# Where the splits of newly loaded weights stand in ScalarE's queue, and the order of the seven products of a hidden block, in a four-layer trunk

## The chip, the cores and the metric

The kernel runs on 1 core of one Trainium2 chip. The metric is the device time of one execution in microseconds (us), the median of the runs; lower is better. TensorE (PE) does the matmuls, VectorE (DVE), ScalarE (ACT) and GpSimd (POOL) the elementwise work, and SyncE (SP) issues most of the loads.

## The reference

The reference is a trunk of two layers, each a half-step SwiGLU feed-forward network (FFN), a mixer (a gated short convolution in the first layer, sparse attention in the second) and another half-step FFN. That makes six stages, numbered s = 0 to 5; stages 0, 2, 3 and 5 are the FFNs. Only they matter here:

```python
def swiglu(h, w_in, w_out):
    g, u = jnp.split(h @ w_in, 2, axis=-1)
    return (jax.nn.silu(g) * u) @ w_out

x = x + HALF * gate[:, 0, None, :] * swiglu(h, ffn_w_in[i, 0], ffn_w_out[i, 0])
```

Here x is 512 positions by 1024, w_in is 1024 by 5632 (2816 for g and 2816 for u) and w_out is 2816 by 1024, all in fp32.

## The kernel before, in words

**Splitting.** An fp32 operand goes through the matmul as two numbers, a high part and a low part. `split` (L163 and L164) makes them: ACT copies the value into the high part, and DVE subtracts that from the value for the low part. A product of two split operands takes three matmuls: high by high (L167), high by low (L168) and low by high (L169); in the rows of the profile the weight is the second name, so that `gu<-hhi,whi` has the weights' high part and `gu<-hhi,wlo` their low part.

**The hidden blocks.** An FFN has 22 hidden blocks of 128, in four groups (0 to 5, 6 to 11, 12 to 17, 18 to 21), called p = 0 to 3 below. Most blocks are done by `seven_products`: a block's two 1024 by 128 weight matrices (g and u) and the 512 positions are cut in halves, so that eight products of blocks become seven of sums of blocks. It is called 73 times: 16 times in the first FFN and 19 times in each of the other three. One call is a *pair* here. A product is 12 matmuls of 128x256 (4 blocks of the inner dimension by 3). Their names, by the stationary operand in the profile's rows:

- `a11` and `a12` take the newly loaded weights, split into `whi` and `wlo`;
- `b2·t2` takes `qbh`/`qbl`, `s1·t1` and `s3·t3` take `qah`/`qal`, the fourth-sum product takes `qdh`/`qdl`, and the last product takes `qch`/`qcl`. The tiles qa, qb and a are sums and quarters of the same weights, split in the same way. Of qb there are two sums, made by DVE at L661 and L662 from the raw weights.

Three PSUM banks of a pair are called gu. Each of them is read once by a copy on ACT in `copied` (L697): `e0` after a11, `e1` after b2·t2, `e3` after s1·t1. The product that next adds to the same bank has to wait for that copy: b2·t2 for e0, s3·t3 for e1, the fourth-sum product for e3. After that DVE adds (L708, L721, L725), ACT applies Silu (L726), and two DVE operations (L731, L732) make the hidden block af, which is split into ahi and alo.

The pairs overlap. A call returns two functions, `fourth` (the fourth-sum product with its add and Silu) and `last` (the last product, L731, L732 and the split of af), which the next call runs among its own products. The steady order on PE, with X for a pair and Y for the next, is: a11 of Y, fourth of X, a12 of Y, b2·t2 of Y, last of X, s1·t1 of Y, s3·t3 of Y. Only the second pair of a group runs fourth ahead of a11.

**Loads and buffers.** The raw weights (`wraw`, 512 KB), their high and low parts have three buffers each, shared with the weights of the output projection and of the next stage. SP issues the loads of raw weights (L656 in a pair, L186 elsewhere).

**After a group.** The group's blocks go through w_out into eight outputs y of 128x512, with weights by `ffn_out` (768 columns, L186), and L813 adds each to x. The first two outputs are begun ahead of the group's last block. The fourth group has no y phase: four weight pairs `ws` (two through the shared buffers, two through other tiles as th and tl) feed the products ty, and the first weights of the next stage are loaded there too (called nx0, of `in_cwi`, `in_ffi` or `in_nwi`).

**What sets the order.** The program is written for a scheduler that puts each engine's instructions in a fixed queue; `tc.high_priority()`, `tc.issue_after(...)` and `behind(...)` steer it. `tc.issue_after(ins)` puts what follows behind ins in a queue; it works on the instructions that ins's own engine gets. So behind a copy on ACT it places the high part and leaves the low part on DVE free. In before, the split of a pair's weights is placed in this way for a group's second pair only, behind the e1 copy of the first. `each` (called in `row` and after L813) gives DVE row sums of another stage's modulation weights (L147) to do beside.

Of the kernel before, what the change touches and what calls it, by code (L numbers as in the profile page):

```python
# [22 lines left out]
P = 128  # L23
# [3 lines left out]
KD = D // P  # L27
# [26 lines left out]
def decoder_kernel(ctx, tc, xT, cT, ng, adaw, adab, ffi, ffo, cwi, cw, cwo,  # L54
                   nwi, nwv, pos, w1, w2, qg, kg, nwo, rb, onehot, rowok, out):
    nc = tc.nc
# [394 lines left out]
        return weights(ffi[f, j, c], KD, P, own, held, to=to)  # L451


    def ffn_out(f, d, m, j0, j1, own=None):
        src = ffo[f, d:d + m, :, j0 * P:j1 * P].rearrange("d p c -> p d c")
        return weights(src, m * (j1 - j0), P, own)

    class Hidden:
        def __init__(self, es, bufs):
# [160 lines left out]
    def ffn(s, f, nrm, nxt, w0, ahead, extra=(), soon=()):  # L620
        with ExitStack() as es:
# [12 lines left out]
            def seven_products(j, later, before, copied_before, second):  # L634
                QT = KD * P // 2
                quart = lambda c, k: ffi[f, j, c].rearrange("p k n -> p (k n)")[:, k * QT:(k + 1) * QT]
                raw = wp.tile([P, 2, QT], F32, name="wraw", tag="wraw", bufs=3)
                whi = wp.tile([P, 2, QT], F32R, name="whi", tag="whi", bufs=3)
                wlo = wp.tile([P, 2, QT], F32R, name="wlo", tag="wlo", bufs=3)
                qa = next(sums)()  # L640
                a22 = tp.tile([P, T], F32, name="a22", tag="nacc", bufs=1) if j == nj and not first else tmp("a22")
                qb = [tmp("qb", tag="sq") for _ in range(2)] if first else swa.tile([P, 2, QT], F32, name="qb")
                qbs = qb if first else [qb[:, 0], qb[:, 1]]
                ah_, al_ = (sw.tile([P, 2, QT], F32R, name=f"qa{e}") for e in "hl")
                b2 = [sw.tile([P, QT], F32R, name=f"qb{e}") for e in "hl"]
                halves = qa if isinstance(qa, list) else [qa[:, 0], qa[:, 1]]
                nc.sync.dma_start(halves[0], quart(0, 0))
                nc.sync.dma_start(halves[1], quart(1, 1))
                a21 = quart(1, 0)
                if qa is halves:  # L650
                    for q in qa:
                        nc.gpsimd.dma_start(q, a21, accum_op=ALU.add)
                else:
                    nc.gpsimd.dma_start(qa, bass.AP(tensor=a21.tensor, offset=a21.offset, ap=[a21.ap[0], [0, 2], a21.ap[1]]),  # L654
                                        accum_op=ALU.add)
                nc.sync.dma_start(raw.rearrange("p a b -> p (a b)"), ffi[f, j, 0].rearrange("p k n -> p (k n)"))  # L656
                nc.sync.dma_start(a22, quart(1, 1))

                def operands(after=nullcontext):
                    with after(), behind(*hid.done) if first and copied_before else nullcontext():  # L660
                        nc.vector.tensor_tensor(qbs[0], halves[1], raw[:, 0], ALU.add)  # L661
                        nc.vector.tensor_tensor(qbs[1], qbs[0], raw[:, 1], ALU.add)  # L662
                    with tc.issue_after(copied_before.ins) if second else nullcontext():
                        split(raw, whi, wlo)
                    if qa is halves:
                        for n, q in enumerate(qa):
                            split(q, ah_[:, n], al_[:, n])
                    else:
                        split(qa, ah_, al_)
                    split(qbs[0], *b2)  # L670

                if j == nj and first:
                    with behind(*held_back):
                        operands()
                elif later:
                    with behind(*hid.done):
                        operands()
                else:
                    operands((lambda: behind(*nrm.done[1])) if j == nj else nullcontext)

                def product(o, w, b, begin=True):
                    for i in range(KD // 2):
                        c = slice(i * P, (i + 1) * P)
                        mh, ml = b(i)
                        mm3(o, w[0][:, c], w[1][:, c], mh, ml, begin and i == 0, i == KD // 2 - 1, skip_group_check=True)

                a11, a12 = [(whi[:, i], wlo[:, i]) for i in range(2)]
                s3, s1 = [(ah_[:, i], al_[:, i]) for i in range(2)]
                t1, t2, t3, t4 = nrm.blocks
                lo, hi = slice(0, HT), slice(HT, T)  # L690
                ox, oy, oz = psum("gu"), psum("gu"), psum("gu")
                e = sw.tile([P, 2, HT], F32, name="e", bufs=2)
                e3 = tmp("e3", HT, "xr")

                def copied(to, o):
                    with tc.high_priority():
                        return nc.scalar.activation(to, o[:, lo], AF.Copy)  # L697

                if second:
                    before[0]()  # L700
                product(ox[:, lo], a11, nrm.quarter(0, 0))
                copied(e[:, 0], ox)
                if not second:
                    before[0]()
                b4 = [sw.tile([P, QT], F32R, name=f"qd{e}") for e in "hl"]
                split(qbs[1], *b4)
                product(oz[:, lo], a12, nrm.quarter(1, 0))
                nc.vector.tensor_tensor(e[:, 0], oz[:, lo], e[:, 0], ALU.add)  # L708
                product(ox[:, lo], b2, t2, begin=False)
                copy = copied(e[:, 1], ox)  # L710
                before[1]()
                if second and late:
                    late.pop()
                    with tc.issue_after(hid.done[1].ins):
                        each()
                c22 = [sw.tile([P, QT], F32R, name=f"qc{e}") for e in "hl"]
                split(a22, *c22)
                product(oy[:, lo], s1, t1)
                copied(e3, oy)
                product(ox[:, lo], s3, t3, begin=False)  # L720
                nc.vector.tensor_tensor(e3, ox[:, lo], e3, ALU.add)  # L721

                def fourth():
                    product(oy[:, lo], b4, nrm.quarter(1, 1), begin=False)
                    nc.vector.tensor_tensor(e[:, 1], oy[:, lo], e[:, 1], ALU.add)  # L725
                    nc.scalar.activation(e, e, AF.Silu)  # L726

                def last():
                    product(ox[:, lo], c22, t4, begin=False)
                    af = tmp("af")  # L730
                    nc.vector.scalar_tensor_tensor(af[:, hi], e[:, 1], -1.0, e3, op0=ALU.mult, op1=ALU.mult)  # L731
                    nc.vector.scalar_tensor_tensor(af[:, lo], e[:, 0], -1.0, ox[:, lo], op0=ALU.mult, op1=ALU.mult)  # L732
                    keep(af)

                return (fourth, last), copy
# [33 lines left out]
                    hid.activate(os[2 * j], os[2 * j + 1])  # L769
            held_back = []  # L770
            copy, late = None, []
            for p, (j0, j1) in enumerate(FOUR):
                rest = none = (lambda: None,) * 2
                for j in range(max(j0, nj), j1):
                    rest, copy = seven_products(j, p and j == j0, rest, copy, copy and j == max(j0, nj) + 1)
                n = j1 - j0
# [13 lines left out]
                if not final:  # L790
                    begun = []
                    for d in range(KD):
                        if d < 2 and both:
                            if not d:
                                a = (hid.hi[j0:j1 - 1], hid.lo[j0:j1 - 1])
                                for dd in range(2):
                                    begun.append((ffn_out(f, dd, 1, j0, j1), psum("y")))
                                    project(begun[dd][1], begun[dd][0], 0, a, [(k, k) for k in range(n - 2)], True, False)
                                    if not dd:
                                        rest[1]()  # L800
                                for w, o in begun:
                                    project(o, w, 0, a, [(n - 2, n - 2)], False, False)
                                a = (hid.hi[j0:j1], hid.lo[j0:j1])
                                row()
                            w, o = begun[d]
                            project(o, w, 0, a, [(n - 1, n - 1)], False, True)
                        else:
                            w = ffn_out(f, d, 1, j0, j1)
                            if first and not p and d == 6:
                                held_back[:] = last_split  # L810
                            o = psum("y")
                            project(o, w, 0, a, [(k, k) for k in range(n)], True, True)
# [802 lines left out]
```

## Time and profile before

| | us |
|---|---|
| runs | 1907.12, 1908.41, 1909.41 (median 1908.41) |
| profiled execution | 1905.69 |
| its span | 1903.9 |
| PE busy | 1871.5 (98%) |
| DVE busy | 1516.9 (80%) |
| ACT busy | 951.1 (50%) |
| mean granted clock | 1.0 |

The span runs from the first to the last instruction on the core; what the execution took beyond it is 1.8 us. A timeline row has the start, the duration, the engine, the line, the operation with its output and inputs, and in square brackets the idle time of the engine ahead of it with what ended it. The matmuls overlap one another, so a row's 0.28 is not what a matmul costs; the distance between two starts is.

### The profile page before, as it was taken

Reading aid. Unit: us, or ns where it says so; the run is one execution under the profiler, and the core shown is the slowest. Engines: PE = TensorE matmul, PEld = TensorE weight load, DVE = VectorE, ACT = ScalarE, POOL = GpSimd, SP = SyncE. Lnnn points to the kernel's source line nnn. Section 1 sums busy time; section 2 is a strip of 40 time slices with the busy share of each in tenths; the row PEclk is TensorE's granted clock in tenths of the full one; section 3 lists DMA queues with packets and bytes.
Section 4 is the critical chain, followed back from the end, with each engine's and each line's share of the span. In section 5 each row is a group of like instructions: output and inputs, shape, how many; then the busy total and the mean of one; then the engine's idle time right before and its main releaser. Section 6 shows DMA issues by size and latency. Waiting matters only on the chain.

```text
span 1903.9 us, 34466 instructions
## 1 busy us (share of the span) xinstructions
PE 1871.5 (98%) x13293; PEld 1736.6 (91%) x13293; DVE 1516.9 (80%) x2792; ACT 951.1 (50%) x1679; POOL 250.5 (13%) x346
## 2 busy tenths in 40 slices
PE   7999999999999999999999999999999999999999
PEld 5989999988899899999989899999888789898989
DVE  8977878887797878788878878887898988585765
ACT  3445344532245454545635353554788856363542
POOL 0011111000011111100011111000454620010100
PEclk9999999999999999999999999999999999999999
DMA  8587767366656677774568676234332325474741
GB/s 326 179 241 188 227 175 252 122 222 243 243 161 172 202 197 230 191 248 107 145 210 216 200 200 211 85 110 130 82 99 80 90 72 143 125 201 115 200 121 63
DMA packets 126674, 324.77 MB, mean 171 GB/s; under 512 B 15515, under 2 KB 16651, under 8 KB 126508
## 3 DMA queue, kind: packets, MB, share of 16 engines
q1 hardware_dynamic: 95196, 242.85, 38.6%
q0 software_dynamic: 31312, 79.71, 18.2%
q8 instruction: 104, 1.70, 0.4%
q14 instruction: 62, 0.51, 0.1%
HBM read 313.85 MB, written 3.15 MB: 166 GB/s over the span
## 4 chain that ended last, share of the span: by engine, by line
PE 84%; DVE 8%; ACT 3%; DMA 2%; issue 2%; SPq 1%; DVEq 0%; ACTq 0%
PE gu L167 13%; PE gu L169 12%; PE gu L168 12%; PE y L167 7%; PE y L168 7%; PE y L169 7%; PE cv L167 2%; PE cv L169 2%; PE cv L168 2%; PE hs L168 2%; PE hs L169 2%; PE hs L167 2%; PE ty L168 2%; PE ty L169 2%; PE ty L167 2%
## 5 line engine op out<-in xcount | busy, mean ns | idle before, releaser
L163 ACT ACTIVATE whi<-wraw 128x1024 fp32r<-128x1024 f32 (+2 forms) x261 | 252.7, 976 | 266.7 <-PE y L168 88.5
L164 DVE TENSOR_TENSOR wlo<-wraw,whi 128x1024 fp32r<-128x1024 f32 (+2 forms) x261 | 294.8, 1134 | 44.8 <-ACT whi L163 44.0
L168 PE MATMUL y<-alo,whi 128*128 128x512 f32 x576 | 224.3, 389 | 0.0
L167 PE MATMUL y<-ahi,whi 128*128 128x512 f32 x576 | 224.3, 389 | 0.0
L169 PE MATMUL y<-ahi,wlo 128*128 128x512 f32 x576 | 224.2, 389 | 0.0
L147 DVE CUSTOM_DVE_ANT_0 adaraw<-adaraw,cond,adabs 128x1024 f32<-128x1024 f32 x144 | 185.6, 1305 | 12.9 <-DMA adaraw<-in_adaw 12.6
L167 PE MATMUL gu<-hhi,whi 128*128 128x256 f32 x696 | 192.9, 277 | 0.0
L169 PE MATMUL gu<-hhi,wlo 128*128 128x256 f32 x696 | 192.5, 277 | 0.0
L168 PE MATMUL gu<-hlo,whi 128*128 128x256 f32 x696 | 192.4, 277 | 0.0
L654 POOL DMA_DIRECT2D qa<-in_ffi x70 | 84.5, 1207 | 697.5 <-DMA qa<-in_ffi 259.4
L167 PE MATMUL gu<-th,qah 128*128 128x256 f32 x584 | 161.5, 276 | 1.4 <-ACT e L697 1.4
L169 PE MATMUL gu<-th,qal 128*128 128x256 f32 x584 | 161.2, 276 | 0.0
L168 PE MATMUL gu<-tl,qah 128*128 128x256 f32 x584 | 161.2, 276 | 0.0
L697 ACT ACTIVATE e<-gu 128x256 f32<-128x256 f32 x219 | 82.5, 377 | 127.5 <-PE gu L169 126.7
L167 PEld LDWEIGHTS gu<-hhi,whi 128*128 128x128 f32 x696 | 130.7, 188 | 1.0 <-DVE af L732 0.4
L168 PEld LDWEIGHTS gu<-hlo,whi 128*128 128x128 f32 x696 | 130.6, 188 | 0.5
L169 PEld LDWEIGHTS gu<-hhi,wlo 128*128 128x128 f32 x696 | 130.7, 188 | 0.0
L169 PEld LDWEIGHTS y<-ahi,wlo 128*128 128x128 f32 x576 | 108.1, 188 | 22.9
L167 PEld LDWEIGHTS y<-ahi,whi 128*128 128x128 f32 x576 | 108.2, 188 | 21.7
L168 PEld LDWEIGHTS y<-alo,whi 128*128 128x128 f32 x576 | 108.1, 188 | 21.5
L167 PEld LDWEIGHTS gu<-th,qah 128*128 128x128 f32 x584 | 109.6, 188 | 1.6 <-ACT e L697 1.6
L169 PEld LDWEIGHTS gu<-th,qal 128*128 128x128 f32 x584 | 109.7, 188 | 0.0
(327 smaller groups left out, 5745.1 us busy)
## 6 DMA issues: line engine op xcount, KB each, us to landing
wraw<-in_ffi SPq DMA_DIRECT2D x103, 512.0 KB, 4.6
adaraw<-in_adaw POOLq DMA_DIRECT2D x79, 512.0 KB, 5.0
qa<-in_ffi SPq DMA_DIRECT2D x146, 256.0 KB, 3.9
wraw<-in_ffo SPq DMA_DIRECT2D x96, 384.0 KB, 4.8
qa<-in_ffi POOLq DMA_DIRECT2D x70, 512.0 KB, 7.0
adaraw<-in_adaw SPq DMA_DIRECT2D x65, 512.0 KB, 4.8
a<-in_ffi SPq DMA_DIRECT2D x73, 256.0 KB, 4.3
wraw<-in_cwi SPq DMA_DIRECT2D x24, 512.0 KB, 5.9
```

The costliest lines, as they stand in the source:

```text
L147: return nc.vector.tensor_tensor_reduce(out=raw, in0=raw, in1=cond, scale=scale, scalar=adabs[:, c:c + 1], op0=ALU.mult, op1=ALU.add, accu ...
L163: act = nc.scalar.activation(hi, src, AF.Copy)
L164: return act, nc.vector.tensor_tensor(lo, src, hi, ALU.subtract)
L167: nc.tensor.matmul(o, sh, mh, start=first, stop=False, **kw)
L168: nc.tensor.matmul(o, sh, ml, start=False, stop=False, **kw)
L169: nc.tensor.matmul(o, sl, mh, start=False, stop=last, **kw)
L654: nc.gpsimd.dma_start(qa, bass.AP(tensor=a21.tensor, offset=a21.offset, ap=[a21.ap[0], [0, 2], a21.ap[1]]), accum_op=ALU.add)
L697: return nc.scalar.activation(to, o[:, lo], AF.Copy)
```

## The change

It has three parts.

1. The split of a pair's weights is placed behind a copy for every pair but a group's first, and that copy is now e3 of the pair before (the last one that a pair has) in place of e1. The weights of the two outputs that are begun ahead of a group's last block (`ffn_out` in `begun`) are placed behind e3 of the group's last pair in the same way.
2. The fourth-sum product of X comes ahead of a11 of Y for every pair.
3. a11 runs its eight matmuls with the high part of the weights first and its four with the low part last.

The lines of `seven_products` behind the changed ones move down by up to three: the copy at L697 is at L700 after.

```diff
-    def ffn_out(f, d, m, j0, j1, own=None):
+    def ffn_out(f, d, m, j0, j1, after=None):
         src = ffo[f, d:d + m, :, j0 * P:j1 * P].rearrange("d p c -> p d c")
-        return weights(src, m * (j1 - j0), P, own)
+        return weights(src, m * (j1 - j0), P, after=after)
...
-                    with tc.issue_after(copied_before.ins) if second else nullcontext():
+                    with tc.issue_after(copied_before.ins) if before is not none else nullcontext():
                         split(raw, whi, wlo)
...
-                def product(o, w, b, begin=True):
-                    for i in range(KD // 2):
-                        c = slice(i * P, (i + 1) * P)
-                        mh, ml = b(i)
-                        mm3(o, w[0][:, c], w[1][:, c], mh, ml, begin and i == 0, i == KD // 2 - 1, skip_group_check=True)
+                def product(o, w, b, begin=True, low_last=False):
+                    n = KD // 2
+                    steps = [(i, e) for i in range(n) for e in range(3)]
+                    if low_last:
+                        steps.sort(key=lambda ie: ie[1] == 2)
+                    for at, (i, e) in enumerate(steps):
+                        nc.tensor.matmul(o, w[e == 2][:, i * P:(i + 1) * P], b(i)[e == 1], start=begin and at == 0,
+                                         stop=at == 3 * n - 1, skip_group_check=True)
...
-                if second:
-                    before[0]()
-                product(ox[:, lo], a11, nrm.quarter(0, 0))
+                before[0]()
+                product(ox[:, lo], a11, nrm.quarter(0, 0), low_last=True)
                 copied(e[:, 0], ox)
-                if not second:
-                    before[0]()
...
-                copy = copied(e[:, 1], ox)
+                copied(e[:, 1], ox)
...
-                copied(e3, oy)
+                copy = copied(e3, oy)
...
-                                    begun.append((ffn_out(f, dd, 1, j0, j1), psum("y")))
+                                    begun.append((ffn_out(f, dd, 1, j0, j1, copy), psum("y")))
```

What stands in the queues shows it at three places. The number behind a name only tells tiles apart.

**The first: a pair in the middle of group p = 2 of the first FFN, on ACT.** The copies of this pair X are e_2444 (e1) and e3_2445; qah_2559, qbh_2561, qdh_2608 and e_2579 belong to the next pair Y, whose raw weights are wraw_2552; wraw_2822 are those of the third pair after X. Before:

```order
L697 ACTIVATE e_2444<-gu_2441 128x256
L163 ACTIVATE qch_2522<-a22_2421 128x512
L163 ACTIVATE whi_2823<-wraw_2822 128x1024
L163 ACTIVATE ahi_2518<-af_2515 128x512
L697 ACTIVATE e3_2445<-gu_2442 128x256
L163 ACTIVATE qah_2559<-qa_2555 128x1024
L163 ACTIVATE qbh_2561<-qb_2557 128x512
L697 ACTIVATE e_2579<-gu_2576 128x256
```

After:

```order
L700 ACTIVATE e_2444<-gu_2441 128x256
L163 ACTIVATE qch_2522<-a22_2421 128x512
L163 ACTIVATE ahi_2518<-af_2515 128x512
L700 ACTIVATE e3_2445<-gu_2442 128x256
L163 ACTIVATE whi_2553<-wraw_2552 128x1024
L163 ACTIVATE qbh_2561<-qb_2557 128x512
L163 ACTIVATE qah_2559<-qa_2555 128x1024
L163 ACTIVATE qdh_2608<-qb_2558 128x512
L700 ACTIVATE e_2579<-gu_2576 128x256
```

Before, the split of a pair three later stands between the copies of X; after, no split of weights does, and the split of the next pair's weights stands behind e3 of X.

**The second: on DVE one pair earlier in the same group, where a row sum (L147) stands.** The add e3_2307 belongs to a pair, and the sums qb and the operands with 2417 to 2427 to the next. Before:

```order
L164 TENSOR_TENSOR alo_2381<-af_2377,ahi_2380 128x512
L147 ISA adaraw_2384,mods_109<-adaraw_2384,cond_80,adabs_87 128x1024
L147 ISA mods_109 128x1
L721 TENSOR_TENSOR e3_2307<-gu_2303,e3_2307 128x256
L661 TENSOR_TENSOR qb_2422<-qa_2420,wraw_2417 128x512
L164 TENSOR_TENSOR qal_2425<-qa_2420,qah_2424 128x1024
L662 TENSOR_TENSOR qb_2423<-qb_2422,wraw_2417 128x512
L164 TENSOR_TENSOR qbl_2427<-qb_2422,qbh_2426 128x512
```

After:

```order
L164 TENSOR_TENSOR alo_2381<-af_2377,ahi_2380 128x512
L147 ISA adaraw_2384,mods_109<-adaraw_2384,cond_80,adabs_87 128x1024
L147 ISA mods_109 128x1
L721 TENSOR_TENSOR e3_2307<-gu_2303,e3_2307 128x256
L661 TENSOR_TENSOR qb_2422<-qa_2420,wraw_2417 128x512
L164 TENSOR_TENSOR wlo_2419<-wraw_2417,whi_2418 128x1024
L662 TENSOR_TENSOR qb_2423<-qb_2422,wraw_2417 128x512
L164 TENSOR_TENSOR qal_2425<-qa_2420,qah_2424 128x1024
L164 TENSOR_TENSOR qbl_2427<-qb_2422,qbh_2426 128x512
```

The low part wlo_2419, which before had been made well ahead, now stands behind the row sum, L721 and L661, and ahead of qal and qbl.

**The third: the last two pairs C and D of the second FFN, on ACT.** e3_9209 is C's; the other copies e_9342 (e0, then e1) and e3_9343 are D's; e_9208 in L726 is C's Silu; whi_9317 is D's weights, whi_9484 and whi_9490 are the two weight pairs `ws` of the output, and whi_9508 is nx0, the first weights of the next stage. Before:

```order
L697 ACTIVATE e3_9209<-gu_9206 128x256
L163 ACTIVATE qah_9322<-qa_9319 128x1024
L697 ACTIVATE e_9342<-gu_9339 128x256
L163 ACTIVATE qdh_9371<-qb_9321 128x512
L726 ACTIVATE e_9208<-e_9208 128x512
L163 ACTIVATE whi_9508<-wraw_9510 128x1024
L697 ACTIVATE e_9342<-gu_9339 128x256
L163 ACTIVATE qch_9420<-a22_9320 128x512
L163 ACTIVATE ahi_9416<-af_9413 128x512
L697 ACTIVATE e3_9343<-gu_9340 128x256
```

After:

```order
L700 ACTIVATE e3_9209<-gu_9206 128x256
L163 ACTIVATE whi_9317<-wraw_9316 128x1024
L163 ACTIVATE whi_9484<-wraw_9486 128x1024
L163 ACTIVATE qah_9322<-qa_9319 128x1024
L163 ACTIVATE qdh_9371<-qb_9321 128x512
L163 ACTIVATE whi_9490<-wraw_9492 128x1024
L700 ACTIVATE e_9342<-gu_9339 128x256
L726 ACTIVATE e_9208<-e_9208 128x512
L163 ACTIVATE whi_9508<-wraw_9510 128x1024
L700 ACTIVATE e_9342<-gu_9339 128x256
L163 ACTIVATE qch_9420<-a22_9320 128x512
L163 ACTIVATE ahi_9416<-af_9413 128x512
```

Four splits of weights now stand between e3 of C and e1 of D, where before there was one. On DVE the low parts stand accordingly; after, the row reads:

```order
L708 TENSOR_TENSOR e_9342<-gu_9341,e_9342 128x256
L731 SCALAR_TENSOR_TENSOR af_9413<-e_9208,e3_9209 128x256
L164 TENSOR_TENSOR wlo_9491<-wraw_9492,whi_9490 128x1024
L164 TENSOR_TENSOR wlo_9509<-wraw_9510,whi_9508 128x1024
L732 SCALAR_TENSOR_TENSOR af_9413<-e_9208,gu_9205 128x256
L164 TENSOR_TENSOR qcl_9421<-a22_9320,qch_9420 128x512
L164 TENSOR_TENSOR alo_9417<-af_9413,ahi_9416 128x512
L164 TENSOR_TENSOR tl0_9503<-qa_9504,th0_9502 128x1024
L721 TENSOR_TENSOR e3_9343<-gu_9339,e3_9343 128x256
```

Before, only wlo_9509 stood between L731 and L732 of C, with L708 between them too; wlo_9491 had been made a pair earlier. Besides, nx0's raw tile takes the buffer that D's raw weights have; before, that of an earlier pair.

More of the change, by code (lines that the diff above doesn't have):

```diff
@@ L771, in ffn @@
             copy, late = None, []
+            none = (lambda: None,) * 2
             for p, (j0, j1) in enumerate(FOUR):
-                rest = none = (lambda: None,) * 2
+                rest = none
                 for j in range(max(j0, nj), j1):
```

## The prediction

> **What bounds the kernel now.** The page comes first. Span, engines, clock and chain:
>
> ```profile
> span 1903.9 us, 34466 instructions
> PE 1871.5 (98%) x13293; PEld 1736.6 (91%) x13293; DVE 1516.9 (80%) x2792; ACT 951.1 (50%) x1679; POOL 250.5 (13%) x346
> PEclk9999999999999999999999999999999999999999
> PE 84%; DVE 8%; ACT 3%; DMA 2%; issue 2%; SPq 1%; DVEq 0%; ACTq 0%
> ```
>
> PE is the bound, busy 98% of the span at full clock, and 84% of the chain. The change takes no matmul away, so it can only act on PE's waits. The waits of PE by line, cut to the products of `seven_products`:
>
> ```profile
> PE gu L167 <- ACT e L697: 2.5, 2, 1.4
> PE gu L169 <- DVE qbl L164: 0.8, 1, 0.8
> ```
>
> There are three such waits, 3.3 us together, in all 73 pairs. That is the whole stock from which a gain can come. The timeline of PE shows what one costs, in the first FFN (the first two rows are six matmuls apart by count, the first and the last) and in the third FFN:
>
> ```profile
> 240.79 0.28 PE L167 MATMUL gu<-hhi,whi 128*128 128x256 f32 x1
> ...
> 241.36 0.28 PE L169 MATMUL gu<-hhi,wlo 128*128 128x256 f32 x1
> 242.72 0.38 PE L167 MATMUL gu<-hhi,qdh 128*128 128x256 f32 x1 [1.09 <-ACT e L697]
> 242.94 0.29 PE L168 MATMUL gu<-hlo,qdh 128*128 128x256 f32 x1
> ...
> 247.07 0.38 PE L169 MATMUL gu<-th,qbl 128*128 128x256 f32 x1 [0.84 <-DVE qbl L164]
> ...
> 942.29 0.39 PE L167 MATMUL gu<-th,qah 128*128 128x256 f32 x1 [1.38 <-ACT e L697]
> 942.51 0.28 PE L168 MATMUL gu<-tl,qah 128*128 128x256 f32 x1
> ...
> 943.66 0.28 PE L169 MATMUL gu<-th,qal 128*128 128x256 f32 x1
> 943.94 0.38 PE L167 MATMUL gu<-hhi,whi 128*128 128x256 f32 x1
> 944.16 0.28 PE L168 MATMUL gu<-hlo,whi 128*128 128x256 f32 x1
> ```
>
> From 240.79 to 241.36 are six matmuls, five steps, so a matmul takes 0.114 us, a product of 12 takes 1.36 and a pair of seven 9.52. Across the first wait, 241.36 to 242.72 is 1.36 in place of 0.114, and the next step is 0.22 in place of 0.114: together 1.36, which is the shown idle time of 1.09 and about 0.27 more for the restart. By that rule the three cost 1.36 + 1.11 + 1.65 = 4.1 us. A wait can also be too short to be shown: 943.66 to 943.94 and on to 944.16 is 0.27 over two plain steps, a restart alone. Why PE waited is in ACT's queue:
>
> ```profile
> 240.82 1.06 ACT L163 ACTIVATE whi<-wraw 128x1024 fp32r<-128x1024 f32 x1 [2.66 <-DMA wraw<-in_ffi]
> 241.79 0.61 ACT L163 ACTIVATE ahi<-af 128x512 fp32r<-128x512 f32 x1
> 242.31 0.36 ACT L697 ACTIVATE e<-gu 128x256 f32<-128x256 f32 x1
> 941.12 0.84 ACT L163 ACTIVATE whi<-wraw 128x768 fp32r<-128x768 f32 x1 [4.33 <-DMA wraw<-in_ffo]
> 941.87 0.37 ACT L697 ACTIVATE e<-gu 128x256 f32<-128x256 f32 x1
> ```
>
> Both times a split of weights that nobody needed yet waited for its load (2.66 and 4.33 us), with the copy that PE needed queued behind it. The loads were slow, by SP's timeline:
>
> ```profile
> 234.12 0.38 SPq L656 DMA_DIRECT2D wraw<-in_ffi  x1
> 933.14 4.84 SPq L186 DMA_DIRECT2D wraw<-in_ffo  x2
> ```
>
> From issue to landing that is 6.7 us (234.12 to 240.82) and 8.0 (933.14 to 941.12).
>
> **What the change removes.** With every pair's split behind e3 of the pair before, and the begun outputs' splits behind e3 of the last pair, no load stands ahead of these copies any more. The two ACT waits go, and the late qbl with them, since it was the follow-up of the first (ACT was late with qbh behind the same split). That is -4.1 us, and -0.5 more for two restarts of 0.27: the one at 943.94, and one that I take to stand as well behind the wait at 242.72. The bounds are 0 (if something else is as late) and -5. What is late next there is worked out now.
>
> **The steady pair.** Let T be the start of s1·t1 of X. After, PE runs s1·t1 at T, s3·t3 at T+1.36, fourth at T+2.72, a11 of Y at T+4.08 with its low part from T+4.99 (eight matmuls later), b2·t2 at T+6.80. For what ACT and DVE do in it I take a pair where a row sum stands, whose s1·t1 starts at 227.87:
>
> ```profile
> 227.87 0.28 PE L167 MATMUL gu<-th,qah 128*128 128x256 f32 x1
> 229.43 0.39 ACT L697 ACTIVATE e<-gu 128x256 f32<-128x256 f32 x1 [0.27 <-PE gu L169]
> 229.23 0.69 DVE L164 TENSOR_TENSOR alo<-af,ahi 128x512 fp32r<-128x512 f32 x1
> 229.83 1.28 DVE L147 CUSTOM_DVE_ANT_0 adaraw<-adaraw,cond,adabs 128x1024 f32<-128x1024 f32 x1
> ...
> 231.04 0.42 DVE L721 TENSOR_TENSOR e<-gu,e 128x256 f32<-128x256 f32 x1
> 231.37 0.68 DVE L661 TENSOR_TENSOR qb<-qa,wraw 128x512 f32<-128x512 f32 x1
> 231.97 1.22 DVE L164 TENSOR_TENSOR qal<-qa,qah 128x1024 fp32r<-128x1024 f32 x1
> 233.11 0.68 DVE L662 TENSOR_TENSOR qb<-qb,wraw 128x512 f32<-128x512 f32 x1
> 233.71 0.68 DVE L164 TENSOR_TENSOR qbl<-qb,qbh 128x512 fp32r<-128x512 f32 x1
> ```
>
> e3 is copied from T+1.56 to T+1.95 and whi follows, 1.06 long (row at 240.82), to T+2.9. The high part is due at T+4.08: 1.2 us to spare, at no cost. The low part takes DVE 1.22. Without a row sum L721 waits for s3·t3 and starts at T+2.9; where wlo goes first it is done at T+4.15 (0.8 to spare), and behind L721 and L661 (the first FFN's order) at 2.9 + 0.33 + 0.60 + 1.22, about T+4.8 (0.2 to spare). Cost nothing, covered by a11's high part and fourth. If that cover is gone, PE waits.
>
> It is gone where a row sum stands in the same place, in the first FFN's groups p = 2 and p = 3. By the rows, L661 gives DVE over at 231.97, T+4.10; wlo ends at T+5.32 where it is due at T+4.99. PE waits 0.33 and restarts for 0.27: 0.6. Behind it come L662 (0.60), qal (1.14) and the 0.68 of qbl, by the distances of the rows: qbl is there at about T+7.65, due at T+6.80 + 0.23 + 0.6 = T+7.63. That wait is 0 to 0.3, so 0.8 each time (bounds 0.6 and 0.9): **+1.6 us** for the two.
>
> The order of a11's matmuls costs nothing: as many matmuls and weight loads as before, and 0.114 each whichever part is loaded. I bound that by 0 from both sides within a run's spread. Moving fourth ahead of a11 costs nothing if e3's copy is done by T+2.72; it is at T+1.95.
>
> **The last two pairs of an FFN.** Here three more splits (two `ws`, one nx0) stand between the copies, and nx0's raw tile takes D's buffer, which is free only once D's low part is made (T+4.15, T being C's s1·t1; T+4.7 in the first FFN). I work it out for the second FFN:
>
> ```profile
> 861.76 0.28 PE L167 MATMUL gu<-th,qah 128*128 128x256 f32 x1
> 865.83 0.42 DVE L721 TENSOR_TENSOR e<-gu,e 128x256 f32<-128x256 f32 x1
> 866.30 0.38 PE L167 MATMUL gu<-th,qch 128*128 128x256 f32 x1
> wraw<-in_ffi SPq DMA_DIRECT2D x103, 512.0 KB, 4.6
> wraw<-in_cwi SPq DMA_DIRECT2D x24, 512.0 KB, 5.9
> wraw<-in_nwi SPq DMA_DIRECT2D x18, 512.0 KB, 4.1
> 336.00:342.00 6.00, 6.00 (x55) 6.00 (x54) 4.75 (x9) 4.16 (x8) 0.00 (x0) 1.00 0.64 202
> 858.00:864.00 6.00, 6.00 (x55) 6.00 (x54) 4.61 (x8) 4.26 (x8) 0.00 (x0) 1.00 0.25 82
> ```
>
> D's s1·t1 was at 861.76, so T is 9.52 earlier, 852.24, and the last product started at 866.30, T+14.06, right behind L721. After, DVE has in a row from T+4.15: L721 0.33, wlo of ws 1.14, qal 1.14, L725 0.33, qdl 0.60, L708 0.33, L731 0.33, the other wlo of ws 1.14, wlo of nx0 1.22. That ends at T+10.7, and L732 of C is behind it, where C's last product ends at T+9.7. From there the chain is L732 0.42, ahi 0.61, e3's copy 0.36, th 1.06, tl 1.22, L721 0.42, 4.1 in all or 3.8 with the 0.06 to 0.1 by which one overlaps the next: L721 is done at T+14.5 and the last product starts 0.45 later than before. That is the floor, if nx0 has landed by then. With the median landing of 4.6 it is issued at T+4.25, lands at T+8.85, its splits take 1.06 + 1.22 to T+11.2, and the loss is 1.05; from there on each us of landing costs one. DMA is quiet there (share 0.25 at 858 to 864), so I take **+0.6**. In the third FFN the load is of `in_nwi`, 4.1: **+0.5**, from 0.45 to 0.8. In the first FFN it is issued 0.55 later, DMA is busier (0.64) and `in_cwi` has a median of 5.9: from 1.05 to 2.15, **+1.5**. The fourth FFN has no next stage: 0.
>
> The Trainium skill ("DMA: Bandwidth & Descriptors", the anatomy of one DMA) gives, for loads issued by GpSimd, a fixed 2.0 us and the bytes at 436 GB/s, an estimate of 3.2 us for 512 KB; by it all three would sit at the floor. The medians of the rows are 0.9 to 2.7 over that, so I keep to the rows.
>
> **The sum.** -4.1 - 0.5 + 1.6 + 0.6 + 0.5 + 1.5 = -0.4 us. On the profiled execution that is 1905.69 - 0.4 = 1905.3, of which 1.8 lie outside the span. The median of the runs shown is 2.7 above the profiled one; with that, 1908.0.
>
> **The rivals.**
> 1. *All gains, no losses.* The scheduler's queues are fixed but my sums of DVE's queue are close (0.33 late, 0.45 late); if loads land in 3 to 4 us and DVE runs ahead a little, no loss appears and the 4.6 go: 1903.8. For it: the runs before scatter by 2.3, and their median is 2.7 above an execution that itself waited for two slow loads, so that others may wait more for such loads, which would go too (I allow 1.1 of the 2.7, to 1902.7). Against it: the row-sum pair is late by its own rows.
> 2. *Slower: nx0's load.* In each of three FFNs its split stands ahead of e1 of D on ACT and of L732 of C on DVE. If it takes as long as the load at 933.14, 8.0 us, the loss is 1.05 + 3.4 = 4.45 each, 13.3 in place of 2.6: +10.7 on the forecast, 1918.7. It decides from 4.3 us more than forecast, that is landings 1.4 us longer than I took them in all three. Against it: the DMA share of 0.25, and that the landing of 8.0 is nearly double the medians.
> 3. *The change does not do what it says:* the waits on ACT come back as waits for the weights themselves, because loads that land late are still late. Against it: the split at 240.82 was for a pair that starts over 10 us later. The gain would be 0 and with the losses of 4.2 it is 1908.4 + 4.2 = 1912.6, just past the edge of no change.
>
> **How the numbers follow.** My forecast has 0.52, rival 1 0.28, rival 2 0.12, rival 3 0.08. A measurement of this kernel can tell 0.2%, 3.8 us, from no change. Faster by more (under 1904.6) is rival 1 and 0.03 of the forecast: 0.31. Slower by more (over 1912.2) is rival 2, 0.02 of the forecast, and half of rival 3, which lies at the edge: 0.18. The same: 0.51. The range goes from rival 1 with its extra, 1902.7, to the forecast with the upper bounds of all unknown costs (0.65 + 0.45 + 0.3 + 0.2) and half the scatter of 2.3, 1910.8, and 1.0 on towards rival 3, 1911.8, so that about 2 in 10 are left out; the forecast's own range is 1906 to 1910.8.
>
> **What would show it.** In the profile after, the waits of PE for ACT e in the pairs should be gone at the places of 242.72 and 942.29. New short waits should stand at L169-type matmuls with wlo (a11's low part) behind the row sums of the first FFN's p = 2 and p = 3, 0.3 each, and the last product of the last pair of the first three FFNs should start 0.5 to 2 us later against T. If no such wait appears, rival 1 holds; if PE waits for e1 of D behind whi with a DMA as releaser, rival 2 does.

## The result, and the profile after

| | before | after |
|---|---|---|
| median of the runs, us | 1907.76 (4 runs) | 1934.47 (4 runs) |
| profiled span, us | 1903.9 | 1934.9 |
| mean granted clock | 1.0 | 0.997 |

The change makes the kernel slower: the ratio is 1.0141, with an interval of 1.0123 to 1.0158, or 26.7 us. The profiled span is 31.0 us longer; the execution it belongs to took 1936.69 us, the longest of the four. The page of after, span and engines:

```profile
span 1934.9 us, 34452 instructions
PE 1883.5 (97%) x13293; PEld 1739.1 (90%) x13293; DVE 1513.8 (78%) x2792; ACT 948.1 (49%) x1679; POOL 250.0 (13%) x346
```

The work is the same; PE waits more. The waits of PE by line, after, cut to the products of the FFNs (us in total, how often, the longest):

```profile
PE y L169 <- DVE wlo L164: 10.3, 7, 1.8
PE y L167 <- ACT ahi L163: 9.7, 7, 3.0
PE y L168 <- DVE alo L164: 2.1, 7, 0.3
PE gu L687 <- DVE e L721: 1.0, 2, 0.5
PE gu L687 <- DVE wlo L164: 0.5, 2, 0.2
```

The three waits on ACT's copies and on qbl that the prediction started from are gone. In their place stand 21 waits, 22.1 us, in `y`: in the output products *between* the groups, a place that the prediction priced at nothing. (The last two rows are the small losses inside the pairs that it did forecast.) The timelines of one such place show the chain, the second group's end in the third FFN. First SP and ACT of before, where the first matmul of y starts at 1044.95:

```profile
1040.11 0.33 SPq L186 DMA_DIRECT2D wraw<-in_ffo  x1
1040.49 2.23 SPq L657 DMA_DIRECT2D a<-in_ffi  x2
...
1049.25 0.63 ACT L163 ACTIVATE qch<-a 128x512 fp32r<-128x512 f32 x1 [3.01 <-PE gu L168]
1049.79 0.62 ACT L163 ACTIVATE ahi<-af 128x512 fp32r<-128x512 f32 x1
```

And after, where it starts at 1062.82, with one row of DVE:

```profile
1060.58 2.30 ACT L163 ACTIVATE whi<-wraw 128x768 fp32r<-128x768 f32 x3
...
1062.44 1.53 SPq L186 DMA_DIRECT2D wraw<-in_ffo  x2
1064.02 0.97 SPq L657 DMA_DIRECT2D a<-in_ffi  x1
...
1067.20 0.42 DVE L732 SCALAR_TENSOR_TENSOR af<-e,gu 128x256 f32<-128x256 f32 x1 [2.05 <-PE gu L687]
...
1071.94 0.63 ACT L163 ACTIVATE qch<-a 128x512 fp32r<-128x512 f32 x1 [7.32 <-DMA a<-in_ffi]
1072.47 0.61 ACT L163 ACTIVATE ahi<-af 128x512 fp32r<-128x512 f32 x1
```

Read from the top. The splits of the output weights are now made at 1060.58, behind e3 of the last pair. Until their low parts are made, the three outputs' weights hold all three raw buffers. SP's next two loads are reloads of these buffers, and nothing is issued before a buffer comes free (the first at 1062.44). Behind them in the queue stands the load of `a`, the quarter of the *next group's first pair*. It is issued 1.2 us after the y products begin, where before it was issued 4.5 us ahead of them, and by the end of ACT's wait it lands 7.9 us later, among the reloads. ACT takes its instructions in a fixed order, and qch, the split of that quarter, stands ahead of ahi. Nobody needs qch for a long time; ahi is needed at once. ACT stands idle for 7.3 us ahead of qch. The tile af is done at 1067.6 (1067.20 and 0.42), and ahi starts at 1072.47: some 4.9 us late, for a load that it has nothing to do with. PE, after:

```profile
1073.14 0.50 PE L167 MATMUL y<-ahi,whi 128*128 128x512 f32 x1 [1.89 <-ACT ahi L163]
1073.95 0.50 PE L168 MATMUL y<-alo,whi 128*128 128x512 f32 x1 [0.30 <-DVE alo L164]
...
1079.53 0.39 PE L168 MATMUL y<-alo,whi 128*128 128x512 f32 x1
1081.71 0.50 PE L169 MATMUL y<-ahi,wlo 128*128 128x512 f32 x1 [1.79 <-DVE wlo L164]
```

The second wait, 8 us on, is a consequence on DVE. Of DVE's rows, before:

```profile
1050.53 0.69 DVE L164 TENSOR_TENSOR alo<-af,ahi 128x512 fp32r<-128x512 f32 x1
1057.96 0.95 DVE L164 TENSOR_TENSOR wlo<-wraw,whi 128x768 fp32r<-128x768 f32 x1
```

and after:

```profile
1072.60 0.69 DVE L164 TENSOR_TENSOR qcl<-a,qch 128x512 fp32r<-128x512 f32 x1 [4.98 <-ACT qch L163]
1073.21 0.68 DVE L164 TENSOR_TENSOR alo<-af,ahi 128x512 fp32r<-128x512 f32 x1
1079.50 1.28 DVE L147 CUSTOM_DVE_ANT_0 adaraw<-adaraw,cond,adabs 128x1024 f32<-128x1024 f32 x1 [0.62 <-DMA adaraw<-in_adaw]
1080.71 0.95 DVE L164 TENSOR_TENSOR wlo<-wraw,whi 128x768 fp32r<-128x768 f32 x1
```

From alo to the low part of the fourth output's weights it is 7.4 us before and 7.5 after: three row sums, two adds and the split of qal in DVE's order. Before, alo was ready about 2 us ahead of PE, and those 7.4 us lay beside matmuls. After, PE resumes right behind ahi and alo, and the part of the 7.5 us that is longer than PE's own work up to that point is a wait.

How often this happens stands in ACT's waits, before and after:

```profile
ACT qch L163 <- DMA a<-in_ffi: 5.7, 1, 5.7
```

```profile
ACT qch L163 <- DMA a<-in_ffi: 65.3, 11, 8.5
```

There are eleven group ends with begun outputs. At each the quarter is issued 4.2 to 4.5 us ahead of the first matmul of y before, and 1.2 to 1.5 us behind it after.

Besides, PE's clock fell. Of the windows by time, after (the last three columns are the granted clock, DMA share and GB/s):

```profile
1070.00:1076.00 6.00, 3.81 (x16) 2.60 (x15) 3.40 (x5) 3.57 (x5) 0.54 (x1) 1.00 0.26 103
1082.50:1086.00 3.50, 3.50 (x10) 2.74 (x9) 2.76 (x4) 0.00 (x0) 0.53 (x1) 0.51 0.93 328
```

Behind the wait at 1081.71 the matmuls run at half clock for some 3.5 us. There are three such stretches, 21 matmuls at 0.43 us in place of 0.23, about 4.2 us. The sum is then 22.1 of waits, about 6 for their restarts (21 of about 0.3) and 4.2 of clock, 32.3 in the outputs; by the starts of PE's rows, the products of the pairs with the last one of each FFN take 1.4 us less than before. That makes 30.9, against 31.0. The clock's part is not in every execution: one of the four, at a mean granted clock of 1.0, took 1933.66 us.

### The profile page after: what moved, and what is told of

It reads as the page before. It is cut to its first block, busy times and chain, and to the rows that moved or that the text cites. A ratio compares the mean times of both kernels' runs of the same rounds, so it can differ in the third digit from the quotient of the medians.

```text
span 1934.9 us, 34452 instructions
## 1 busy us (share of the span) xinstructions
PE 1883.5 (97%) x13293; PEld 1739.1 (90%) x13293; DVE 1513.8 (78%) x2792; ACT 948.1 (49%) x1679; POOL 250.0 (13%) x346
## 4 chain that ended last, share of the span: by engine, by line
PE 72%; DVE 12%; issue 6%; DMA 6%; ACT 3%; SPq 0%; POOL 0%; DVEq 0%; ACTq 0%; POOLq 0%
PE gu L687 28%; PE y L169 5%; PE y L168 5%; PE y L167 5%; DVE wlo L164 2%; PE cv L167 2%; PE cv L168 2%; PE cv L169 2%; DMA qa<-in_ffi 2%; PE hs L168 2%; PE hs L169 2%; PE hs L167 2%; DMA adaraw<-in_adaw 2%; DMA a<-in_ffi 2%; PE ty L168 1%
## 5 line engine op out<-in xcount | busy, mean ns | idle before, releaser
L147 DVE CUSTOM_DVE_ANT_0 adaraw<-adaraw,cond,adabs 128x1024 f32<-128x1024 f32 x144 | 184.4, 1297 | 10.3 <-DMA adaraw<-in_adaw 10.1
L700 ACT ACTIVATE e<-gu 128x256 f32<-128x256 f32 x219 | 83.1, 379 | 191.1 <-PE gu L687 191.1
L687 PE MATMUL gu<-hhi,whi 128*128 128x256 f32 x584 | 151.2, 277 | 0.0
L687 PE MATMUL gu<-hlo,whi 128*128 128x256 f32 x584 | 151.1, 277 | 0.0
L687 PE MATMUL gu<-hhi,wlo 128*128 128x256 f32 x584 | 126.9, 278 | 0.5 <-DVE wlo L164 0.5
L163 ACT ACTIVATE qbh<-qb 128x512 fp32r<-128x512 f32 x73 | 46.2, 633 | 137.6 <-PE gu L687 84.0
L687 PEld LDWEIGHTS gu<-hhi,whi 128*128 128x128 f32 x584 | 109.6, 188 | 0.5
L687 PEld LDWEIGHTS gu<-hlo,whi 128*128 128x128 f32 x584 | 109.6, 188 | 0.5
```

What stands on the lines that cost most here:

```text
L147: return nc.vector.tensor_tensor_reduce(out=raw, in0=raw, in1=cond, scale=scale, scalar=adabs[:, c:c + 1], op0=ALU.mult, op1=ALU.add, accu ...
L163: act = nc.scalar.activation(hi, src, AF.Copy)
L687: nc.tensor.matmul(o, w[e == 2][:, i * P:(i + 1) * P], b(i)[e == 1], start=begin and at == 0, stop=at == 3 * n - 1, skip_group_check=True)
```

## The experiments

The theory, called S below: the late split holds the raw buffers, SP's queue stands at their reload, the quarter `a` behind it is late, and ahi is late because it stands behind qch. The rivals are that all pairs' splits do this, that ACT's own work or a crowded DMA does it, that the order of the products does it, or that row sums do. Each ratio is to the kernel before on the same chip, with its 95% interval.

**1. The begun outputs' splits free again.**

```diff
-    begun.append((ffn_out(f, dd, 1, j0, j1, copy), psum("y")))
+    begun.append((ffn_out(f, dd, 1, j0, j1), psum("y")))
```

> The changed kernel with one edit undone: the splits of the two outputs that are begun early are not placed behind e3 of the group's last pair. Theory S (these splits, made 8 us later, keep the raw buffers; SP's queue stands behind them, a22 of the next group's first pair lands late, and qch and ahi with it): the waits of y for ahi (9.7), alo (2.1) and wlo (10.3) go and about 33 us of PE's time at the group ends with them; what is left are the gains and the small losses inside the pairs, 1903 to 1909 us. Rival P (the splits of all pairs behind e3 keep the raw buffers, and that alone makes the loads late): still over 1925.

Measured: 1907.69 us against 1906.74, ratio 1.0009 (1.0000 to 1.0019). No wait of y for ahi, alo or wlo of the FFNs is left, and qch waits for its load once (5.2 us), as before. The pairs' splits and the order of the products together cost next to nothing: the rivals of all pairs' splits and of the order fall. What the begun outputs' placement was meant to remove is back: six waits of PE for ACT's copies, 2.1 us, the longest (0.54, at 270.8) behind a split that waited 2.9 us for its load.

**2. The kernel before with this edit alone.** The begun outputs' splits are placed behind e3 of the last pair:

```diff
-    copied(e3, oy)
+    third = copied(e3, oy)
...
-    begun.append((ffn_out(f, dd, 1, j0, j1), psum("y")))
+    begun.append((ffn_out(f, dd, 1, j0, j1, third), psum("y")))
```

> The kernel before with this one edit alone: the splits of the two begun outputs behind e3 of the group's last pair; pairs and products as before. Theory S: the same waits at the group ends as in the changed kernel, 25 to 33 us over before less the 1.65 of the wait at 942, 1930 to 1940 us. Rival P: 1906 to 1909, since no pair's split moves.

Measured: 1923.99 us, ratio 1.0098 (1.0080 to 1.0115), 17.3 us. The edit alone makes most of the loss, but less than expected. Its waits of PE and ACT:

```profile
PE y L169 <- DVE wlo L164: 13.1, 8, 1.8
```

```profile
ACT qch L163 <- DMA a<-in_ffi: 61.3, 12, 6.2
```

The same place on SP and ACT, where the first matmul of y starts at 1057.6:

```profile
1058.82 0.42 SPq L657 DMA_DIRECT2D a<-in_ffi  x1
1065.62 0.63 ACT L163 ACTIVATE qch<-a 128x512 fp32r<-128x512 f32 x1 [6.21 <-DMA a<-in_ffi]
```

qch waits twelve times here, but at most 6.2 us where it was 8.5; ahi is late enough for DVE's chain to stand open, and seldom late enough to stop PE by itself (1.1 us in two waits). The quarter is issued as late as in the changed kernel, 1.2 us behind the first matmul of y; it lands 6.8 us later in place of 7.9. That the two parts of the change add more than their sum is what the runs show; which other loads make the landing slower in the changed kernel was not separated.

**3. The quarter loaded by GpSimd's queue**, in all 73 pairs.

```diff
-    nc.sync.dma_start(a22, quart(1, 1))
+    nc.gpsimd.dma_start(a22, quart(1, 1))
```

> The changed kernel with the loads of a22 issued by GpSimd in place of SP, so that they no longer stand behind the raw weights in SP's queue; all else the same. Theory S: qch no longer waits for a22 at the group ends; the waits of y for ahi and alo go, and most of those for wlo, which follow: 1906 to 1916. Rival A (it is not the load: three splits behind e3 fill ACT and DVE, so that ahi and alo are late by the work itself): 1930 to 1936, ahi as late as now.

Measured: 1937.89 us, ratio 1.0169 (1.0152 to 1.0186). The expectation missed: it got slower still. The trace tells why. Its waits, and the same place on GpSimd and ACT:

```profile
PE y L167 <- ACT ahi L163: 19.0, 7, 3.8
PE y L169 <- DVE wlo L164: 5.1, 4, 1.6
```

```profile
1060.97 1.21 POOL L654 DMA_DIRECT2D qa<-in_ffi  x1 [7.84 <-DVE e L721]
1061.72 1.62 POOL L657 DMA_DIRECT2D a<-in_ffi  x2
```

```profile
1071.87 0.63 ACT L163 ACTIVATE qch<-a 128x512 fp32r<-128x512 f32 x1 [9.03 <-DMA a<-in_ffi]
```

GpSimd's queue has a stop of its own, the accumulating load of qa, and the quarter, issued behind it at 1061.72, lands 10 us later. qch waits 9.0 us there in place of 7.3, and PE's waits for ahi grow from 9.7 to 19.0. This doubled the wait for ahi in place of taking it away. It fits the last link, qch ahead of ahi, and says nothing on SP's queue.

**4. qch behind ahi, the load as late as it was.**

```diff
-    split(a22, *c22)
+    with tc.issue_after(hid.done[0].ins) if later else nullcontext():
+        split(a22, *c22)
```

> The changed kernel with the split of a22 of a group's first pair placed behind ahi of the last block of the group before; the loads stay where they are in SP's queue and come as late as now. Theory S (the late load costs only because qch stands ahead of ahi): y's waits for ahi and alo go, those for wlo at least to a third: 1906 to 1914. If instead the late load costs by itself (row sums, the next pair): 1920 or more.

Measured: 1909.33 us, ratio 1.0015 (1.0006 to 1.0024): some 24 of the 27 us are back with one split placed behind another at each group end. PE's wait in y that is left, ACT's wait for the load, and DVE at the same place:

```profile
PE y L169 <- DVE wlo L164: 5.3, 6, 1.3
ACT qch L163 <- DMA a<-in_ffi: 13.8, 7, 5.5
```

```profile
1057.31 0.69 DVE L164 TENSOR_TENSOR qcl<-a,qch 128x512 fp32r<-128x512 f32 x1 [1.22 <-ACT qch L163]
1057.91 0.75 DVE L815 SCALAR_TENSOR_TENSOR x<-y,mods,x 128x512 f32<-128x512 f32 x1
...
1061.70 0.95 DVE L164 TENSOR_TENSOR wlo<-wraw,whi 128x768 fp32r<-128x768 f32 x1
```

The late quarter now seems to stop DVE at qcl, with the adds, the row sums and wlo behind it. At the place shown the profile names a matmul as what ended ACT's wait for qch, at others the load; run 5 tests it.

**5. qch and qcl behind the last output's split.** The same edit with `last_split[0].ins`, the split of the weights of the eighth output on ACT, in place of `hid.done[0].ins`.

> The changed kernel with the split of a22 of a group's first pair placed behind the split of the last output's weights on ACT, so that neither qch on ACT nor qcl on DVE stands ahead of anything that the outputs need. Theory S: in the run with qch behind ahi the remaining waits of y for wlo (5.3, six times, 6.9 with their restarts) are qcl standing in DVE's queue until a22 has landed (1057.31 in that run, ahead of the add of x0); they go: 1909.3 - 6.9 = 1902.4, 3 to 6 us under the kernel before. Rival: those waits come from the row sums, whose own loads are late; then 1907 to 1910.

Measured: 1904.26 us against 1907.91, ratio 0.9984 (0.9975 to 0.9992), 3.1 us faster than the kernel before. Of the waits of y for wlo, two are left:

```profile
PE y L169 <- DVE wlo L164: 0.9, 2, 0.6
```

So it was the quarter's split, qcl on DVE, and not the row sums' own loads.

**6. The kernel before with that placement alone.**

> The kernel before with the same placement of the first pair's a22 split and nothing else. Theory S: in it a22 has landed long before qch's turn, so nothing is gained: within 2 us of the kernel before. If the placement is a gain of its own, 3 us or more faster.

Measured: 1905.99 us, ratio 0.9995 (0.9986 to 1.0003). No difference that can be told: in before a matmul, and not the load, ends ACT's wait for qch. Run 5, measured on the same chip, is 1.7 us faster still (1904.26 against 1905.99), so most of its gain belongs to the change; about 1.0 us, which is within the noise here, may be the placement's own.

**7. The order of the products alone.** The kernel before with parts 2 and 3 of the change.

> The kernel before with the order of the products alone changed (fourth ahead of a11 for every pair, a11's low part last); all splits placed as before. The prediction's price for this is 0: 1904 to 1909. If the order itself costs something on PE or moves queues so that the y phase is late, over 1912.

Measured: 1912.58 us, ratio 1.0026 (1.0016 to 1.0035), 5.0 us slower, just past the point set for it. The price of 0 holds only beside part 1. ACT's timeline in the first FFN:

```profile
241.61 1.06 ACT L163 ACTIVATE whi<-wraw 128x1024 fp32r<-128x1024 f32 x1 [1.61 <-DMA wraw<-in_ffi]
242.58 0.61 ACT L163 ACTIVATE ahi<-af 128x512 fp32r<-128x512 f32 x1
243.10 0.36 ACT L700 ACTIVATE e<-gu 128x256 f32<-128x256 f32 x1
```

The split that waits for its load still stands ahead of e3, and with fourth ahead of a11 there is one product less between the copy and the product that needs it: PE waits for ACT's copies seven times, 4.8 us, where it was twice, 2.5. With five more restarts of 0.27 that is some 3.7 of the 5.0 us; the rest was not followed up.

**8. The pairs' splits behind e3, the order of the products as in before.** The begun outputs' splits are free.

> The placement of the pairs' splits behind e3 alone, with the products in their old order and the begun outputs' splits free. In the old order a11 starts at T+2.72, when whi is there at T+2.9, and its third matmul at T+2.95 needs wlo, there at T+4.15 at the earliest. By the prediction's account the product order is the cover: without it PE waits about 1.2 to 1.8 us and a restart in nearly each of 57 pairs (all but a group's first): 80 to 120 us, 1985 to 2030. If ACT and DVE run ahead enough without it, 1906 to 1912.

Measured: 1928.09 us, ratio 1.0105 (1.0089 to 1.0121), 20.1 us slower: the right sign, a quarter of the size. PE's timeline of a pair:

```profile
1034.77 0.28 PE L169 MATMUL gu<-th,qal 128*128 128x256 f32 x1
1035.11 0.39 PE L167 MATMUL gu<-hhi,whi 128*128 128x256 f32 x1
1035.34 0.28 PE L168 MATMUL gu<-hlo,whi 128*128 128x256 f32 x1
1035.46 0.28 PE L167 MATMUL gu<-hhi,qdh 128*128 128x256 f32 x1
```

The scheduler did not leave PE standing at the third matmul: it ran two matmuls of a11, then nine of the fourth product, then the rest of a11. So mainly the wait for whi remains, 0.34 and 0.23 where 0.114 is the step: a third of a us in 43 pairs, some 15 of the 20 us. Six waits for ACT's copies, 1.6 us, and smaller ones make the rest. The order of the products is the cover for the late splits, as the prediction had it, but the scheduler finds most of that cover by itself.

**9. The quarter ahead of the reloads in SP's queue.** Its load is written ahead of the last block; no split moves, and qch stays ahead of ahi:

```diff
+    if not final:
+        early_a22.append(tmp("a22"))
+        nc.sync.dma_start(early_a22[0], ffi[f, j1, 1].rearrange("p k n -> p (k n)")[:, KD * P // 2:])
     rest[0]()
```

> The changed kernel with the load of a22 of a group's first pair written ahead of the group's last block, so that it stands ahead of the two reloads of raw weights in SP's queue that wait for the begun outputs' splits; qch stays ahead of ahi on ACT and no split moves. Theory S (the late split holds the raw buffers, SP stands at the reload, and a22 behind it is late): a22 lands before qch's turn, the waits of y for ahi and alo go to under 2 us, those for wlo to under 6: 1904 to 1912. Rival (a22 is late because DMA is crowded there, or because of ACT's own work): waits of y as now, over 1925.

Measured: 1904.96 us against 1905.93, ratio 0.9997 (0.9987 to 1.0006). The same place on SP and ACT:

```profile
1036.82 0.91 SPq L782 DMA_DIRECT2D a<-in_ffi  x1
1043.49 1.53 SPq L186 DMA_DIRECT2D wraw<-in_ffo  x2
```

```profile
1048.17 0.64 ACT L163 ACTIVATE qch<-a 128x512 fp32r<-128x512 f32 x1 [2.51 <-PE gu L688]
1048.71 0.63 ACT L163 ACTIVATE ahi<-af 128x512 fp32r<-128x512 f32 x1
```

The quarter is issued 6.7 us ahead of the reloads, and its landing no longer ends ACT's wait for qch; a matmul does. The waits of y for ahi and alo are gone, 0.5 us for wlo is left. That the loads land faster there is not the reason. Of the twelve early ones:

```profile
DMA to landing us min/median/max: 4.8/7.2/7.5
```

A median of 7.2 us is about the 7.9 of the changed kernel. This is the run that tells SP's queue apart: the begun outputs' splits stand 2.2 us ahead of the first matmul of y as in the changed kernel, ACT has the same work in the same order, and only the load's place in the queue differs.

**10. Both mends together** (9 and the placement of 5).

> Both mends together: the changed kernel with a22 of a group's first pair loaded ahead of the reloads, and its split behind that of the last output's weights. By theory S each alone takes the same waits away (y for ahi and wlo had 0.5 us left with the early load and 0.9 with the late split), so together they give no more than one of them: 1903 to 1906, 1 to 5 under the kernel before. If the two gains add up, under 1902.

Measured: 1904.44 us against 1906.44, ratio 0.9990 (0.9981 to 0.9999). As expected the two do not add: each removes the same waits. It is the fastest profiled span of all, 1901.9 us, but among runs 5, 9 and 10 these measurements don't choose.

## Why the prediction was wrong, point by point

- **The waits that go.** Right. The three waits of 3.3 us are absent from the profile after, and no wait of PE for ACT's copies took their place.
- **The step that failed** stands in the same paragraph: "the begun outputs' splits behind e3 of the last pair" were booked as a gain alone. Their slack was asked of the product that needs them, and never of the buffers that they read. For nx0 the prediction did follow a raw buffer to its reload; for the begun outputs it did not. A split is the last reader of its raw tile, so making it later made every load behind that tile's reload in SP's queue late: run 9 against the changed kernel, a ratio of 0.9997 in place of 1.0141, some 27 us for one load's place. The second half of the miss is the order on ACT: that qch of the next group stands ahead of ahi was true before and harmless, because its load was early.
- **The row-sum pairs.** Right in mechanism and place, too high in size: two waits of PE for wlo, 0.5 us in all as shown, about 0.5 each with the restarts, where 0.8 was forecast and 0.6 was the lower bound. The second, on qbl, did not come.
- **The last two pairs.** In the second and third FFN the last product waits 0.66 in place of 0.23 us over a plain step, 0.43 more, close to the floor of 0.45; forecast were 0.6 and 0.5. In the first FFN, forecast at 1.5, the last product is no later than before (0.23), and only two short waits of about 0.3 stand there, for D's low part and for e0. The slow landing was not met. (In the working, splits done at T+11.2 against T+10.7 make 0.95 and not 1.05, and for the first FFN its own terms, 0.55 of issue and 1.3 of landing more, go to 2.8 and not 2.15.)
- **The sum.** With the one load mended (run 9) the change is worth -0.6 us, from -2.5 to 1.1, where the working had -0.4 for all that it looked at. That the two are so close is in part luck: the losses that it added up to 4.2 came to about 2.5 (1.0, 0.9 and 0.6), and the interval is wide beside the difference. What it looked at was not far off; what decided was outside it.
- **The rivals.** The slower rival put the loss at the last two pairs of an FFN and at nx0's load. The mechanism was of that kind, a load released late with a split that PE needs queued behind it, but at the group ends and not at the last pairs. The first rival, all gains and no losses, falls with the waits of the row-sum pairs. The third, waits for the weights themselves in place of those on ACT, does not show: no wait of a pair's product for a high part stands in the table of after.
- **The order of the products at 0.** Too simple: alone it costs 5.0 us (run 7). Beside part 1, where no split stands ahead of e3, it costs nothing that can be told (run 1).

## What to carry to other kernels

When an instruction is moved later, look up what it *reads* and when that buffer is loaded again: the reload and everything behind it in the same queue move with it. Then ask, on the engine that works on what those loads bring, which instruction that waits for a late load stands ahead of one that is urgent. Here the mend was either of two lines: the load ahead of the reloads, or the patient split behind the urgent one.

## What the runs showed of the hardware that had not been expected

The clock fell after short waits. At 1081.71 in the changed kernel PE had waited 1.79 us, and 1.89 us some 8 us earlier; from 1082.9 on eight matmuls took 0.43 us each in place of 0.23, at a granted clock of 0.51. The Trainium skill ("TensorE: Matmul & The Clock Gate", Part 1, the clock gate) has the clock halved after an idle window of about 3.4 us; this trace shows it halved behind a wait of about half that. Not every such wait did it: behind the 1.89 at 1073.14 the clock stayed at 1.00. The other two stretches came behind waits of 3.03 us (724.4) and 1.72 (1169.4). Together the three made about 4 of the 31 us; what decides which wait does it, these runs don't show.
